# An MLP with more block products, every instruction in a planned order, 23 shared weight buffers, and sums and residual in DRAM

## The chip, the cores and the metric

The program runs on one core of a Trainium2 chip. The metric is the device time of the whole program in microseconds, as a median of several runs.

The engines are named as the profile names them: PE multiplies matrices, DVE (VectorE) and ACT (ScalarE) do elementwise work, POOL (GpSimd) does a little of it and can issue DMAs, and SP issues nearly all DMAs.

## What is computed

Two layers of a transformer with 256 tokens and width 2048. The attention parts (banded, stick-breaking and memory attention) are untouched by the change. The MLP of each layer is

```python
def sq_relu_mlp(h, g, w_in, w_out):
    return jnp.square(jax.nn.relu(rms_norm(h, g) @ w_in)) @ w_out

h = h + jnp.concatenate([y_main, y_mem], axis=-1) @ w_o[layer]
h = h + sq_relu_mlp(h, norm_mlp[layer], w_mlp_in[layer], w_mlp_out[layer])
```

with a hidden width of 8192. All data are float32.

## The kernel before

**Precision.** Each float32 factor is split into a part `hi` in PE's fp32r format and the rest, `lo`. A product is the sum of hi x hi, hi x lo and lo x hi. Each weight unit is a raw tile of 128 x 1024 that SP loads; ACT casts it to `hi` and DVE subtracts to get `lo` (`parts` L168, `prepare` L230). Pools give six raw, four hi and five lo buffers, and the units are prepared at most `AHEAD + 1` = 4 ahead of PE.

**The MLP in turns** (`mlp`, L985). The hidden width is cut into four chunks of 2048. PE's work is a list of steps (`mlp_steps`, L54, from the strings in `TURNS`):

- **U f** is one tile of 128 hidden features of the up product (`features_major`, L378 on): 16 wide matmuls (512 columns) with hi and 16 narrow ones (256 columns) with lo, into one PSUM bank. Then ACT copies the low half (L449), DVE adds (L1174), applies the relu and the norm (L1156), ACT squares (L1159), and the result is split into `hid`.
- **A j and B j** are direct steps of the down product, for one pair j of hidden tiles and one half (A or B) of a group's output columns: 12 wide matmuls each. They need one weight unit.
- **S j** does the work of A j and B j together by seven block products in place of eight (`Sevenfold`, `prepare_seven` L202, `Group.seven` L1084): 21 wide matmuls. For it, DVE forms block differences of the raw weights (L220 to L224, four of 512 columns) and of the hidden tile (`block_sums`, L1117), and ACT and DVE split four units, one of which is half as wide.

A group is one half of the output columns for a chunk: n = 0 or 1. The first three chunks have both groups in this form, the last one only n = 0; its other two column blocks are plain down products after it (L1240). `SEVEN = 5`: five of the eight pairs of every group are S steps, three are A and B.

A group holds seven of the eight PSUM banks until its sums are complete; one is left for U steps. When a bank is complete, `Group.add` (L1066) adds it to a sum in SBUF: an addition of 512 columns on DVE (L1082), or an ACT copy in the first chunk (L1080). At the end `merged` (L1016) adds the product sums to the four output sums of the group with six additions, and `turned` (L999) transposes the result on PE and adds it to the residual `h`, which stays in SBUF from the first out projection to the end. In the second layer the transposes of column block 3 come first, soon after the last S, A and B steps.

**What sets the order.** PE's order is the program's. On the other engines the framework's scheduler places the instructions by its own estimate, so a step's preparation runs beside earlier steps. Persistent tiles, heads and sums share a pool of 13 buffers (`grp`, L129).

The functions that the change touches, and those that call them:

Of the kernel before, what the change touches and what calls it, by code (L numbers as in the profile page):

```python
# [9 lines left out]
F32 = mybir.dt.float32  # L10
# [27 lines left out]
AHEAD = 3  # L38

# [14 lines left out]
def mlp_steps():  # L54

    steps = [(0, 0, "H", 0)] + [(0, 0, "T", f) for f in range(FIRST_UP, ALONE, 2)]
    for c in range(NCH):
        for n in range(2 if c < NCH - 1 else 1):
            for step in TURNS[n].split():
                kind, i = step[0], int(step[1:])  # L60
                steps.append((c + 1 if kind == "U" and n == 1 else c, n, kind, i))
    return steps


class InOrder:
# [5 lines left out]
    def __getattr__(self, name):  # L71
        fn = getattr(self._engine, name)

        def call(*args, **kwargs):
            return self._tc.keep_in_program_order(fn(*args, **kwargs))  # L75

        return call

# [17 lines left out]
class Engines:  # L96
    def __init__(self, tc):
        nc = tc.nc
        self.tensor = InOrder(tc, nc.tensor)
        self.vector, self.scalar, self.gpsimd, self.sync = nc.vector, nc.scalar, nc.gpsimd, nc.sync  # L100
# [3 lines left out]
def trunk(  # L104
# [97 lines left out]
    def prepare_seven(i, seven):  # L202
# [19 lines left out]
        elif seven.step == 3:  # L222
            nc.vector.tensor_tensor(b11, b22, b11, op=ALU.add)  # L223
            nc.vector.tensor_tensor(b21, b21, b11, op=ALU.subtract)  # L224
# [345 lines left out]
    def normed_heads(banks, eps_ms, gain, dst, wait=2):  # L570
# [24 lines left out]
        def side():  # L595
# [3 lines left out]
            for m in range(2):  # L599
# [11 lines left out]
                )  # L611

# [11 lines left out]
    def heads4(name):  # L624
        return grp.tile([P, 1024], F32, name=name, tag="g4")

# [156 lines left out]
    def load_tokens(src, name, queue):  # L783
        chunks = []
        for c in range(4):
            t = heads4(f"{name}{c}")
            pin(queue.dma_start(t[:], src[c]))
            chunks.append(t)
# [28 lines left out]
    def mlp_stream(l):  # L817
# [5 lines left out]
        for c, n, kind, i in mlp_steps():  # L823
# [115 lines left out]
    km, vm = [], []  # L939

    for l, mg in enumerate((mg0, mg1)):
# [10 lines left out]
        def keys(b, wait, k_=k_, g=g):  # L952

            late = 2 + wait
            later(lambda: normed_heads(b, mstat["em"], sm[:, g : g + 1], k_[:], late), wait)
# [10 lines left out]
        else:  # L966
            tokens_major(mg, lambda b: keys(b, 0))
            tokens_major(mg, lambda b: value_heads(b, mstat["r"], vm[1]))
# [16 lines left out]
    def mlp(l, xg_, sq, h, done):  # L985
        start_side(delayed(inverse_root(sq, f"mlp{l}"), 4))
        sums = [heads4(f"d{l}_{i}") for i in range(4)]
# [5 lines left out]
        extra = [heads4(f"e{l}_{i}") for i in range(3)]  # L993

        def product_sum(i, n):

            return extra[i][:, n * 512 : (n + 1) * 512]
# [18 lines left out]
        def merged(n):  # L1016

            u, p5, p7 = (product_sum(i, n) for i in range(3))
            for i, (dst, src) in enumerate((
                (summed(0, 2 * n + 1), u),  # L1020
                (summed(0, 2 * n + 1), p5),
                (u, p7),
                (summed(1, 2 * n), u),
                (u, p5),
                (summed(1, 2 * n + 1), u),
            )):
                pin(nc.vector.tensor_tensor(dst, dst, src, op=ALU.add))
# [10 lines left out]
        sevens = SEVEN  # L1038

        class Group:  # L1040

            def __init__(self, c, n, factors, staged=None):
                self.c, self.factors, self.staged = c, factors, staged
                self.banks = {}
# [5 lines left out]
                self.sums_of = {  # L1050
                    "11": [summed(0, 2 * n)], "21": [summed(1, 2 * n)],
                    "12": [summed(0, 2 * n + 1)], "22": [summed(1, 2 * n + 1)],
                    "p1": [product_sum(0, n), summed(0, 2 * n)], "p6": [product_sum(0, n)],
                    "p5": [product_sum(1, n)], "p7": [product_sum(2, n)],
                }
# [10 lines left out]
            def add(self, q, a, w):  # L1066
                count = self.counts[q]
                product(self.bank(q), a, w, count)
                if count[0] < count[1]:
                    return  # L1070
                src = self.banks[q][:]
                if self.staged is not None and q in ("12", "22", "p1", "p5", "p6", "p7"):

                    copy = wide.tile([P, 512], F32, name="copy", tag="wide")
                    nc.scalar.copy(copy[:], src)
                    self.staged.extend((dst, copy[:]) for dst in self.sums_of[q])
                    return
                for dst in self.sums_of[q]:
                    if self.c == 0 and q not in ("11", "p6"):
                        nc.scalar.copy(dst, src)  # L1080
                    else:
                        nc.vector.tensor_tensor(dst, src, dst, op=ALU.add)  # L1082

            def seven(self, j):  # L1084
                s = self.factors[j]
                width["last"] = "wide"
                for step, pairs in enumerate((
                    (("p1", s[0]), ("11", tokens(2 * j + 1, 0))),
                    (("12", s[4]),),
                    (("p5", s[1]), ("p7", s[3])),  # L1090
                    (("p6", s[2]), ("21", tokens(2 * j + 1, 1))),
                )):
                    w = weights()
                    for k2, (q, a) in enumerate(pairs):
                        self.add(q, a, part(w, k2))
                    if step in (1, 3):
                        slot()

            def direct(self, j, col):
                width["last"] = "wide"  # L1100
                w = weights()
                for m in range(2):
                    for k2 in range(2):
                        self.add(f"{m + 1}{col}", tokens(2 * j + k2, m), part(w, k2))
                slot()
# [11 lines left out]
        def block_sums(c, j, a, b):  # L1117

            whole = c == NCH - 1
            s23 = nar.tile([P, T], F32, name="s23", tag="nar")  # L1120
            s14 = nar.tile([P, T], F32, name="s14", tag="nar")
            a11, a21, a12, a22 = a[:, :P], a[:, P:], b[:, :P], b[:, P:]
            s1 = s14[:, :P] if whole else a21
            w = wide.tile([P, 512], F32R, name="s_w", tag="wide")
            if not whole:
                x = nar.tile([P, T], F32R, name="s_x", tag="bias", bufs=6)
                last = (x[:, :P], x[:, P:], s14[:, P:])
            elif j < 2:
                x = wide.tile([P, 512], F32R, name="s_x", tag="wide")
                last = (x[:, :T], x[:, T:], s14[:])  # L1130
            else:
                x = [nar.tile([P, T], F32R, name="s_x", tag="bias", bufs=6) for _ in range(2)]
# [298 lines left out]
```

## Time and profile before

| | us |
|---|---|
| median of 3 runs (2158.17 to 2159.33) | 2158.41 |
| the profiled execution | 2158.02 |
| its span, first to last instruction | 2156.3 |
| PE busy | 2148.9 |
| DVE busy | 1745.1 |
| ACT busy | 1248.3 |
| POOL busy | 205.5 |

The granted PE clock is 1.00 over the whole span. In the profile's rows a line such as L174 is the place in the kernel that issued the instruction, `out<-in` are the program's tiles, `x32` the count; after the bar stand the busy time of the group, the mean of one in ns, and the time that the engine was idle just before them with what ended the idle time. In a row of windows every engine has its busy time in that stretch with its number of instructions. All matmuls have one line, L75, since a helper issues them: the tiles tell them apart. Those of U read `mlpx`, those of the down product `hid`, `s_w` and `s_x`.

### The profile page before, as it was taken

The page shows a single profiled execution, that of the slowest core. Times are in us where ns is not written, and L with a number is a line of the kernel's source. Part 1 is how long each engine was busy: PE and PEld are TensorE (multiplying, and loading weights), DVE is VectorE, ACT ScalarE, POOL GpSimd, SP SyncE. Part 2 cuts the span into 40 slices and gives each one's busy share as a digit, 9 for nine tenths or more (in the row PEclk, how much of TensorE's full clock was granted, in tenths as well). Part 3 has the DMA queues.
Part 4 walks back from the last instruction along what each step waited for, and adds up shares of the span by engine and source line. Part 5 has one row for each costly group of instructions (what it writes and reads, how often), then busy time and mean ns, then how long its engine had stood idle before and what let it go on. Part 6 is the DMA issues. An engine that isn't in the chain of part 4 may idle for free.

```text
span 2156.3 us, 30341 instructions
## 1 busy us (share of the span) xinstructions
PE 2148.9 (100%) x11038; PEld 1841.2 (85%) x11038; DVE 1745.1 (81%) x2603; ACT 1248.3 (58%) x1828; POOL 205.5 (10%) x223
## 2 busy tenths in 40 slices
PE   9999999999999999999999999999999999999999
PEld 8888888888888888888888889888888888888887
DVE  7778885679898899989986556566988888988995
ACT  7744545556666566566555547655666656556663
POOL 0010112610000000000050112252000000000000
PEclk9999999999999999999999999999999999999999
DMA  9655556656666756666766654455666666666674
GB/s 331 193 165 187 167 180 195 196 188 187 192 200 200 214 180 197 205 199 196 215 177 194 187 187 137 131 184 184 185 214 186 197 205 200 202 194 205 186 224 128
DMA packets 213317, 414.65 MB, mean 192 GB/s; under 512 B 13232, under 2 KB 144304, under 8 KB 213168
## 3 DMA queue, kind: packets, MB, share of 16 engines
q1 hardware_dynamic: 212592, 410.63, 62.0%
q8 instruction: 86, 1.41, 0.3%
q10 hardware_dynamic: 576, 2.10, 0.3%
q14 instruction: 63, 0.52, 0.1%
HBM read 410.58 MB, written 2.10 MB: 191 GB/s over the span
## 4 chain that ended last, share of the span: by engine, by line
PE 98%; DVE 2%; issue 0%; ACT 0%; DVEq 0%
PE acc L75 93%; PE accs L75 1%; PE yp L75 1%; PE tp L75 1%; PE s L75 1%; PE z L75 1%; DVE lo L226 0%; PE cold L75 0%; DVE lo L174 0%; DVE pt L654 0%; DVE lo L248 0%; ACT hi L171 0%; DVE h L1011 0%; PE stat L75 0%; DVE raw L223 0%
## 5 line engine op out<-in xcount | busy, mean ns | idle before, releaser
L174 DVE TENSOR_TENSOR lo<-raw,hi 128x1024 fp32r<-128x1024 f32 (+1 forms) x524 | 642.5, 1237 | 220.9 <-ACT hi L171 194.8
L171 ACT CAST hi<-raw 128x1024 fp32r<-128x1024 f32 (+1 forms) x524 | 539.2, 1045 | 339.2 <-PE acc L75 286.0
L75 PE MATMUL acc<-mlpx,hi 128*128 128x512 f32 x2048 | 483.9, 389 | 0.0
L75 PE MATMUL acc<-hi,hid 128*128 128x512 f32 x1404 | 474.4, 391 | 0.0
L75 PEld LDWEIGHTS acc<-mlpx,hi 128*128 128x128 f32 x2048 | 383.6, 188 | 79.3
L225 ACT CAST hi<-raw 128x1024 fp32r<-128x1024 f32 (+1 forms) x280 | 264.8, 946 | 204.9 <-DVE raw L221 132.8
L226 DVE TENSOR_TENSOR lo<-raw,hi 128x1024 fp32r<-128x1024 f32 (+1 forms) x280 | 302.0, 1087 | 34.6 <-ACT hi L225 29.5
L75 PEld LDWEIGHTS acc<-hi,hid 128*128 128x128 f32 x1404 | 264.0, 188 | 52.6
L75 PE MATMUL acc<-lo,hid 128*128 128x512 f32 x702 | 274.5, 391 | 0.0
L75 PEld LDWEIGHTS acc<-mlpx,lo 128*128 128x128 f32 x2048 | 261.3, 191 | 9.0
L75 PE MATMUL acc<-mlpx,lo 128*128 128x256 f32 x2048 | 264.6, 283 | 0.0
L75 PE MATMUL acc<-hi,xg 128*128 128x512 f32 x640 | 208.4, 398 | 0.0
L75 PEld LDWEIGHTS acc<-lo,hid 128*128 128x128 f32 x702 | 132.3, 188 | 23.2
L247 ACT CAST hi<-raw 128x1024 fp32r<-128x1024 f32 x108 | 113.4, 1055 | 65.2 <-PE acc L75 54.6
L449 ACT COPY low<-acc 128x256 f32<-128x256 f32 x188 | 69.4, 369 | 136.1 <-PE acc L75 135.0
L75 PEld LDWEIGHTS acc<-hi,xg 128*128 128x128 f32 x640 | 120.2, 188 | 24.6
L248 DVE TENSOR_TENSOR lo<-raw,hi 128x1024 fp32r<-128x1024 f32 x108 | 131.0, 1230 | 6.1 <-ACT hi L247 6.1
L75 PE MATMUL acc<-lo,xg 128*128 128x512 f32 x320 | 124.7, 390 | 0.7 <-DVE lo L174 0.7
L75 PE MATMUL acc<-y,hi 128*128 128x512 f32 x512 | 119.9, 391 | 0.0
L75 PEld LDWEIGHTS acc<-y,hi 128*128 128x128 f32 x512 | 95.0, 188 | 19.1
L75 PE MATMUL acc<-hi,s_w 128*128 128x512 f32 x280 | 97.6, 389 | 0.0
L1159 ACT ACTIVATE up<-up 128x256 f32<-128x256 f32 x128 | 52.8, 415 | 40.2 <-DVE up L1156 40.2
(211 smaller groups left out, 2612.6 us busy)
## 6 DMA issues: line engine op xcount, KB each, us to landing
raw<-in_w_up SPq DMA_DIRECT2D x256, 512.0 KB, 4.8
raw<-in_w_down SPq DMA_DIRECT2D x256, 512.0 KB, 6.0
raw<-in_w_in SPq DMA_DIRECT2D x80, 512.0 KB, 3.9
raw<-in_w_o SPq DMA_DIRECT2D x64, 512.0 KB, 4.2
raw<-in_w_mem SPq DMA_DIRECT2D x28, 512.0 KB, 5.8
raw<-in_w_kv_v SPq DMA_DIRECT2D x24, 512.0 KB, 4.1
raw<-in_w_kv_k SPq DMA_DIRECT2D x24, 512.0 KB, 4.4
raw<-in_w_q SPq DMA_DIRECT2D x24, 512.0 KB, 4.2
```

What stands on the lines that cost most here:

```text
L75: return self._tc.keep_in_program_order(fn(*args, **kwargs))
L171: nc.scalar.copy(hi[:, :n], raw[:, :n])
L174: nc.vector.tensor_tensor(lo, raw, hi.bitcast(F32), op=ALU.subtract)
L225: nc.scalar.copy(hi4, src)
L226: nc.vector.tensor_tensor(lo4, src, hi4.bitcast(F32), op=ALU.subtract)
L247: nc.scalar.copy(hi4, turned)
L248: nc.vector.tensor_tensor(lo4, turned, hi4.bitcast(F32), op=ALU.subtract)
L449: nc.scalar.copy(low[:], bank[:, T:])
L1159: nc.scalar.activation(a[:], a[:], AF.Square)
```

## The change

**More block products.** `SEVEN` is now a table: seven pairs of eight in the first three chunks of both layers, five in the last. The turns for seven are `U S0 U S1 ... U S6 A7 B7` and the like. In each layer six groups have 7 S, 1 A and 1 B in place of 5 S, 3 A and 3 B. Nine U steps (before: ten) come ahead of the first S.

**An order planned by deadlines.** From the first of these steps to the last, nothing is issued as the code meets it. Each instruction becomes a `Job` with an engine, a cost, a due time and what it waits for. `in_turn` walks through the plan: PE, POOL and SP take their jobs in order; ACT and DVE take the job with the earliest due time among those that are ripe. The jobs are then issued in that order and every engine is held to it (`nc.use(nc.tied)`).

**23 shared buffers.** A raw, hi or lo tile no longer has its own pool: six raw, four hi, five lo and eight more buffers from `grp` serve any of the three. The half-wide unit of an S step keeps hi and lo in one buffer.

**Sums and residual in DRAM.** A complete bank is copied to SBUF by ACT. Two such copies fill a tile, which POOL sends by DMA to its sum in DRAM, adding there from the second chunk on. In the last chunk POOL brings the eight sums back into eight of the shared buffers, and DVE adds the last banks to them; `merged` has eight additions now. The residual goes to DRAM after each out projection and comes back in the last chunk; the second layer's memory keys and values do the same between their making and their use. `grp` has nine buffers instead of thirteen, and a second tag of four (`h4`) holds the residual or the copies.

The core of the diff:

```diff
-SEVEN = 5
-ALONE = 10
-TURNS = (
-    "U10 S0 U11 S1 U12 A5 S2 U13 S3 U14 A6 S4 U15 B5 B6 A7 B7",
-    "U0 S0 U1 A5 U2 S1 U3 A6 U4 S2 U5 A7 U6 S3 U7 S4 U8 B5 U9 B6 B7",
-)
+SEVEN = [[7, 7, 7, 5], [7, 7, 7, 5]]
+ALONE = 9
+TURNS = {
...
+    7: (
+        "U S0 U S1 U S2 U S3 U S4 U S5 U S6 A7 B7",
+        "U S0 U S1 U S2 U S3 U S4 U S5 U S6 U A7 U B7",
+    ),
+}
...
+def in_turn(jobs, slots, counts, reserve=RESERVE):
...
+    queues = {e: [job for job in jobs if job.engine == e] for e in ("PE", "POOL", "ACT", "DVE", "SP")}
+    for e in ("ACT", "DVE"):
+        queues[e].sort(key=lambda job: job.key)
...
+                look = queue[:1] if e in ("PE", "POOL", "SP") else queue[:160]
+                job = next((x for x in look if can(x, now)), None)
...
-    grp = ctx.enter_context(tc.tile_pool(name="grp", bufs=13))
+    grp = ctx.enter_context(tc.tile_pool(name="grp", bufs=9))
...
+    away = ctx.enter_context(tc.tile_pool(name="away", bufs=10, space=bass.MemoryType.DRAM))
...
+    def put_away(tile_, name):
+
+        home = away.tile([P, 1024], F32, name=f"away_{name}", tag="away")
+        nc.gpsimd.dma_start(home[:], tile_[:])
+        return home
...
-                for dst in self.sums_of[q]:
-                    if self.c == 0 and q not in ("11", "p6"):
-                        nc.scalar.copy(dst, src)
-                    else:
-                        nc.vector.tensor_tensor(dst, src, dst, op=ALU.add)
...
+            def copy_out():
+                if (id(homes), k) not in g.copies:
+                    g.copies[id(homes), k] = kept4("copy")
+                i = place(q, n)[1]
+                nc.scalar.copy(
+                    g.copies[id(homes), k][:, i * 512 : (i + 1) * 512], g.banks[q][:]
+                )
...
+            def send():
+                if c == 0:
+                    nc.gpsimd.dma_start(out=homes[k][:], in_=g.copies[id(homes), k][:])
+                else:
+                    nc.gpsimd.dma_start(
+                        out=homes[k][:], in_=g.copies[id(homes), k][:], accum_op=ALU.add
+                    )
...
+        slots = [("g4", m) for m in range(SPARE)] + [("raw", m) for m in range(6)]
+        slots += [("hi", m) for m in range(n_given, 4)] + [("lo", m) for m in range(n_given, 5)]
+        counts = {"acc": 4, "t": 1, "y": 1, "nar": 6, "wide": 7, "bias": 6, "copy": COPIES, "s": 2}
...
+        order = in_turn(jobs, slots, counts)
+        nc.use(nc.tied)
+        for job in order:
+            job.emit()
+        nc.use(nc.free)
```

Three places show how instructions move. The first is DVE shortly after the planned part begins in the first MLP. Before (`raw` and `lo` are weight tiles, `up<-acc` takes the bank of a U step, `4x128` is a block difference of weights):

```order
L1174 TENSOR_TENSOR up<-acc,low 128x256
L226 TENSOR_TENSOR lo_4814<-raw_0_4710,hi_4813 128x1024
L174 TENSOR_TENSOR lo_4829<-raw_4827,hi_4828 128x1024
L1156 SCALAR_TENSOR_TENSOR up<-up,ri_mlp_4388 128x256
L174 TENSOR_TENSOR lo_4839<-raw_4837,hi_4838 128x1024
L1115 TENSOR_TENSOR s_x<-s_4753,s_x 128x128
L226 TENSOR_TENSOR lo_4856<-raw_0_4851,hi_4855 128x1024
L226 TENSOR_TENSOR lo_4869<-raw_1_4853,hi_4868 128x512
L1115 TENSOR_TENSOR hid_4160<-up,hid_4160 128x256
L220 TENSOR_TENSOR raw_1_4853<-raw_1_4853 128x4x128
L221 TENSOR_TENSOR raw_1_4853<-raw_1_4853,raw_0_4851 128x4x128
L223 TENSOR_TENSOR raw_0_4851<-raw_1_4853,raw_0_4851 128x4x128
```

Now, up to the lo that the last product of S1 needs (`raws`, `his`, `los` and `g4s` are the shared buffers, each of which may hold a raw, a hi or a lo tile):

```order
L194 TENSOR_TENSOR s_4843<-up 128x128
L194 TENSOR_TENSOR hid_4175<-up,hid_4175 128x256
L194 TENSOR_TENSOR s_4864<-up,s_4843 128x128
L194 TENSOR_TENSOR g4s_1_4866<-g4s_4_4680,los_0_4812 128x1024
L194 TENSOR_TENSOR s_w<-s_4843,s_w 128x256
L194 TENSOR_TENSOR s_x<-s_4864,s_x 128x128
L194 TENSOR_TENSOR g4s_4_4680<-g4s_5_4682,g4s_4_4680 128x4x128
L194 TENSOR_TENSOR g4s_4_4680<-g4s_4_4680 128x4x128
L194 TENSOR_TENSOR up<-acc,low 128x256
L194 TENSOR_TENSOR los_1_4906<-g4s_5_4682,his_1_4890 128x1024
L194 TENSOR_TENSOR his_2_4913<-g4s_6_4684,g4s_0_4826 128x1024
L194 TENSOR_TENSOR g4s_1_4923<-g4s_4_4680,los_0_4911 128x1024
```

The lo units of U and S no longer come in the order of the steps but mixed, and the block differences of the hidden tile (`s`, `up` with 128 columns) stand between block differences of weights.

The second place is DVE at the end of the planned part of the second MLP, from the last banks of the direct steps on. Before (`d` and `e` are the sums in SBUF, `copy` a bank that ACT has copied; `h<-tp` comes soon after):

```order
L248 TENSOR_TENSOR lo_19943<-raw_19941,hi_19942 128x1024
L1082 TENSOR_TENSOR d_0_13872<-acc,d_0_13872 128x512
L1082 TENSOR_TENSOR d_2_13874<-acc,d_2_13874 128x512
L1027 TENSOR_TENSOR e_0_13876<-e_0_13876,e_1_13877 128x512
L1186 TENSOR_TENSOR d_0_13872<-d_0_13872,copy 128x512
L248 TENSOR_TENSOR lo_19965<-raw_19963,hi_19964 128x1024
L1027 TENSOR_TENSOR d_3_13875<-d_3_13875,e_0_13876 128x512
L1186 TENSOR_TENSOR d_0_13872<-d_0_13872,copy 128x512
L1186 TENSOR_TENSOR d_2_13874<-d_2_13874,copy 128x512
```

Now, from the second bank of A7 on (`sum` are the sums brought back from DRAM; one lo and the last addition to `sum_3` follow before the transposes):

```order
L194 TENSOR_TENSOR sum_2_20049<-acc,sum_2_20049 128x512
L194 TENSOR_TENSOR los_1_20398<-los_2_20338,los_0_20394 128x1024
L194 TENSOR_TENSOR sum_1_20240<-sum_1_20240,sum_2_20257 128x512
L194 TENSOR_TENSOR sum_3_20400<-sum_3_20400,sum_2_20257 128x512
L1406 TENSOR_TENSOR sum_0_19953<-sum_0_19953,copy 128x512
L194 TENSOR_TENSOR sum_1_20240<-sum_1_20240,sum_3_20400 128x512
L377 TENSOR_TENSOR lo_20432<-raw_20430,hi_20431 128x1024
L1406 TENSOR_TENSOR sum_2_20049<-sum_2_20049,copy 128x512
L194 TENSOR_TENSOR sum_1_20240<-sum_1_20240,sum_2_20257 128x512
L194 TENSOR_TENSOR sum_3_20400<-sum_3_20400 128x512
L194 TENSOR_TENSOR sum_3_20285<-sum_3_20285,sum_3_20400 128x512
L194 TENSOR_TENSOR sum_3_20400<-sum_3_20400,sum_2_20257 128x512
```

Most of the merge of the four product sums stands behind these banks now, and the transposes that read the result come after it.

The third place is POOL between the last out projection's work and the end of the first MLP. Before, no instruction of POOL lies in the MLP: squares of the residual (`sq`, `mlpsq`) are followed by those after the MLP (`kvsq`):

```order
L977 TENSOR_TENSOR low_4145<-low,h_3211 128x256
L481 TENSOR_TENSOR sq<-h_3211 128x256
L482 TENSOR_TENSOR mlpsq_3214<-mlpsq_3214,sq 128x256
L553 TENSOR_TENSOR root<-ms,neg_half 128x4
L478 TENSOR_TENSOR kvsq<-h_3205 128x256
L481 TENSOR_TENSOR sq<-h_3205 128x256
L482 TENSOR_TENSOR kvsq<-kvsq,sq 128x256
L481 TENSOR_TENSOR sq<-h_3205 128x256 x2
L482 TENSOR_TENSOR kvsq<-kvsq,sq 128x256 x2
L481 TENSOR_TENSOR sq<-h_3207 128x256 x2
```

Now (`away` is the residual in DRAM, `d` and `e` are the sums in DRAM, `copy` a pair of banks):

```order
L764 DMA away_h_3_4165<-h_3217 128x1024
L611 TENSOR_TENSOR mlpsq_3220<-mlpsq_3220,sq 128x256
L682 TENSOR_TENSOR root<-ms,neg_half 128x4
L194 DMA e_0_4171<-copy 128x1024
L194 DMA e_1_4172<-copy 128x1024
L194 DMA d_0_4167<-copy 128x1024
L194 DMA d_2_4169<-copy 128x1024
L194 DMA e_2_4173<-copy 128x1024
L194 DMA e_3_4174<-copy 128x1024
L194 DMA d_1_4168<-copy 128x1024
L194 DMA d_3_4170<-copy 128x1024
L194 DMA e_0_4171<-copy 128x1024
```

Eight DMAs per chunk stand in POOL's queue, and after them those that bring the residual and the sums back.

More of the change, by code (lines that the diff above doesn't have):

```diff
@@ L1 @@
+import heapq
 from collections import deque
@@ new lines, with __init__ @@
+CAST = {128: 300, 256: 405, 512: 623, 1024: 1053}
+SUM = {128: 280, 256: 415, 512: 685, 1024: 1222}
+LOW, SQUARE, COPY = 370, 415, 596
+OVERLAP = {"DVE": 85, "ACT": 75}
+TOLD = 60
+WIDE, NARROW, DRAIN = 227, 120, 200
+ISSUE = {"SP": 60, "POOL": 860}
+LANDS, MOVES, ADDS = 3400, 1690, 2600
+SOON = 200
+class Job:
+    def __init__(self, engine, cost, emit, key, after=(), take=0, give=(), get=(), free=(), adds=False, kinds="g4 raw hi lo"):
+        self.engine, self.cost, self.emit, self.key = engine, cost, emit, key
+        self.after = [job for job in after if job is not None]
+        self.take, self.give, self.get, self.free = take, give, get, free
+        self.adds, self.begun, self.told = adds, None, None
+        self.slots, self.tiles, self.kinds = [], [], kinds.split()
@@ L1066, in add @@
             def add(self, q, a, w):
[L1067 to L1077, printed above, removed]
-                for dst in self.sums_of[q]:
-                    if self.c == 0 and q not in ("11", "p6"):
-                        nc.scalar.copy(dst, src)
-                    else:
[L1082 to L1105, printed above, removed]
+                product(self.bank(q), a, w, self.counts[q])
         def tokens(kt, m):
@@ new lines, in add_job @@
+        def add_job(*args, **kwargs):
+            job = Job(*args, **kwargs)
+            jobs.append(job)
+            return job
+        costs = {"U": 16 * (WIDE + NARROW), "S": 21 * WIDE, "A": 12 * WIDE, "B": 12 * WIDE}
+        begins, now = [], 0
+        for _, _, kind, _ in steps:
+            begins.append(now)
+            now += costs[kind]
+        begins.append(now)
+        next_up = [
+            next((begins[m] for m in range(k + 1, len(steps)) if steps[m][2] == "U"), begins[-1])
+            for k in range(len(steps))
+        ]
@@ new lines, in add_slots, with pe @@
+        def add_slots(*slots):
+            return Held(list(slots))
+        groups = {}
+        ready_at = {}
+        last_pe, bring = None, []
+        alone = min(SEVEN[l][0], ALONE // 2)
+        held = {(0, m): ["wide", "bias"] for m in range(alone)}
+        merge = merged(1)
+        def pe(cost, emit, key, after, give=(), get=(), free=()):
+            nonlocal last_pe
+            last_pe = add_job("PE", cost, emit, key, after, give=give, get=get, free=free)
+            return last_pe
@@ new lines, in mlp @@
+            count([q for q, _ in pairs], end + 2500)
+            if (c, kind, i) == (NCH - 1, "B", KT // 2 - 1):
+                before = None
+                for m in range(4):
+                    after = [returned[id(hs), kk] for hs, kk in sum_homes[4:]]
+                    before = add_job(
+                        "DVE", 2 * SUM[512], lambda: next(merge, None), begins[k] - 9000 + 3000 * m,
+                        [*after, before],
+                    )
+                add_job("POOL", 0, lambda: bring_h(3), begin, [before], get=("copy",))
```

650 lines of the change are left out of this document (555 added, 95 removed).

## The prediction

> **What bounds the kernel now.** First the page's busy shares and its chain of waits, then TensorE's own waits.
>
> ```profile
> PE 2148.9 (100%) x11038; PEld 1841.2 (85%) x11038; DVE 1745.1 (81%) x2603; ACT 1248.3 (58%) x1828; POOL 205.5 (10%) x223
> PE 98%; DVE 2%; issue 0%; ACT 0%; DVEq 0%
> PE tp L75 <- DVE h L1011: 2.2, 2, 1.1
> PE cold L75 <- DVE zeros L142: 1.1, 1, 1.1
> PE acc L75 <- DVE lo L174: 0.7, 1, 0.7
> ```
>
> PE is never without work: 4.0 us of waits in the whole run, and the chain that ends last is PE for 98%. A matmul taken away shortens the run by its interval, as long as PE still finds its operands ready. The intervals are read from PE's timeline inside the first MLP: a U step is one feature tile of the up product, A5 a direct step, and what begins at 666.32 an S step.
>
> ```profile
> 641.49 3.79 PE L75 MATMUL acc<-mlpx,hi 128*128 128x512 f32 x16
> 645.11 2.08 PE L75 MATMUL acc<-mlpx,lo 128*128 128x256 f32 x16
> 647.02 0.40 PE L75 MATMUL acc<-hi,hid 128*128 128x512 f32 x1
> ...
> 649.77 3.79 PE L75 MATMUL acc<-mlpx,hi 128*128 128x512 f32 x16
> ...
> 666.32 0.40 PE L75 MATMUL acc<-hi,hid 128*128 128x512 f32 x1
> ...
> 671.11 3.79 PE L75 MATMUL acc<-mlpx,hi 128*128 128x512 f32 x16
> ```
>
> U takes 647.02 - 641.49 = 5.53 us, a direct step 2.75 us for 12 matmuls, an S step 4.79 us for 21. One wide matmul is 0.228 us.
>
> The next engine is DVE. One chunk period in the middle of the MLP, by windows and by groups within it:
>
> ```profile
> core 0: us, PE busy (x) PEld busy (x) DVE busy (x) ACT busy (x) POOL busy (x), PEclk, DMA share, GB/s
> 788.00:957.52 169.52, 169.52 (x868) 145.07 (x867) 155.04 (x221) 101.93 (x143) 0.00 (x0) 1.00 0.64 199
> L226 DVE TENSOR_TENSOR lo<-raw,hi 128x1024 fp32r<-128x1024 f32 x30 | 36.6, 1220 | 2.7 <-ACT hi L225 2.0 <-PE acc L75 0.5
> L248 DVE TENSOR_TENSOR lo<-raw,hi 128x1024 fp32r<-128x1024 f32 x12 | 14.4, 1218 | 0.0
> L221 DVE TENSOR_TENSOR raw<-raw,raw 128x512 f32<-128x512 f32 x10 | 6.9, 692 | 0.3
> L226 DVE TENSOR_TENSOR lo<-raw,hi 128x512 fp32r<-128x512 f32 x10 | 6.9, 686 | 0.9 <-ACT hi L225 0.8
> L1082 DVE TENSOR_TENSOR d<-acc,d 128x512 f32<-128x512 f32 x10 | 6.7, 684 | 1.0 <-PE acc L75 1.0
> L1082 DVE TENSOR_TENSOR e<-acc,e 128x512 f32<-128x512 f32 x8 | 5.4, 684 | 0.5 <-PE acc L75 0.5
> L1115 DVE TENSOR_TENSOR s_w<-s,s_w 128x256 fp32r<-128x256 f32 x5 | 2.1, 418 | 0.0
> L1140 DVE TENSOR_TENSOR s<-up,s 128x128 f32<-128x128 f32 x5 | 1.4, 287 | 0.0
> ```
>
> DVE works 155.0 of 169.5 us, 91%; a period has 16 U, 10 S and 12 direct steps. How DVE's records lie behind one another decides what is left, so its timeline:
>
> ```profile
> 861.89 2.36 DVE L174 TENSOR_TENSOR lo<-raw,hi 128x1024 fp32r<-128x1024 f32 x2
> 864.17 1.82 DVE L226 TENSOR_TENSOR lo<-raw,hi 128x1024 fp32r<-128x1024 f32 x2
> 866.02 0.69 DVE L220 TENSOR_TENSOR raw<-raw 128x512 f32<-128x512 f32 x1
> 866.75 0.69 DVE L221 TENSOR_TENSOR raw<-raw,raw 128x512 f32<-128x512 f32 x1
> ```
>
> Two independent 1024-wide subtractions start 1.14 us apart (861.89 to 864.17 for two) though each record is 1.22 us: independent neighbours overlap by 0.08 us. Those that touch each other's data don't (866.02 to 866.75, 0.73 us for a record of 0.69).
>
> **PE: what goes.** Per layer, six groups go from five S steps and six direct ones to seven and two: +12 S, -24 direct. An S costs 21 matmuls, the two direct steps that it replaces 24. So 24 x 3 = 72 matmuls of 0.228 us go: 16.4 us, all on the path. The order of PE's instructions has 72 matmuls less. The profiled execution took 2158.02 us (0.4 below the median 2158.41): 2158.0 - 16.4 = 2141.6 if nothing new waits.
>
> **DVE: what it has to do in the shorter period.** Four S more: each three 1024-wide subtractions (1.220), one 512-wide (0.686) and four block differences (0.69), 7.11 us, together +28.4. Eight direct units less: 8 x 1.218 = -9.7. All 18 additions of L1082 go, since ACT now copies the banks out and DMAs add in DRAM: -12.3. Two pairs more of block sums of the hidden tile, each four 128-wide at 0.287 and two splits of 0.418 and about 0.287: +3.7. Sum +10.1; of the 18 instructions more some overlap, -0.9: DVE needs about 164.2 us in a period of 169.5 - 12 x 0.228 = 166.8 us, 98%. That is the weak point: 2.6 us of slack instead of 14.5. Six such periods run (three chunks, two layers).
>
> In the middle of the MLP I price this at nothing. The cover is the lead: by the order, where DVE takes the bank of a U step, the next lo that it has not yet made is used two PE steps, about 10 us, after that U; before, it was sometimes 3.6 us, in the same count.
>
> At the entry the lead is not yet built. From U8's bank to the lo of the last product of S1, DVE's order (the change, first place) has eight 1024-wide (1.14), ten 512-wide (0.61), eight 256-wide (0.34) and six 128-wide (0.2) instructions, 19.1 us with neighbours overlapped, some 0.5 us for those that don't overlap, and 0.7 us until the bank can be added: 20.3. PE passes U9, S0, U10 and 15 matmuls of S1 in 5.53 + 4.79 + 5.53 + 3.42 = 19.3 us, so it waits about 1.0 us, and by the same count about 0.9 more until the middle of the chunk. Taken: 1.9 us per layer, 3.8 in all; bounds 0 (DVE a little quicker than its rows) and 8 (twice that).
>
> At the end of the second MLP the transposes of group 3 follow two units after the last direct step. DVE must do fourteen instructions between A7's second bank and them (the change, second place): three at 1.14 and eleven at 0.61, 10.1 us, and some 0.4 for dependent ones; PE has 3 x 2.75 = 8.2 us. Before, five of them stood between. PE waits 2.4 us. In the first MLP the first transposes come after six units, 7 x 2.75 = 19.2 us behind that bank, and 22 instructions (six at 1.14, sixteen at 0.61, 1 us for dependent ones, 17.6) fit: 0. Taken: 2.4; bounds 0 and 8.
>
> **ACT.** It gains four S (three casts and a short one each), loses eight casts, and copies 16 banks.
>
> ```profile
> L225 ACT CAST hi<-raw 128x1024 fp32r<-128x1024 f32 x30 | 31.6, 1053 | 26.9 <-DVE raw L221 19.8 <-PE acc L75 4.4 <-DVE raw L224 2.4
> L225 ACT CAST hi<-raw 128x512 fp32r<-128x512 f32 x10 | 6.2, 624 | 3.4 <-PE acc L75 3.3
> L1080 ACT COPY d<-acc 128x512 f32<-128x512 f32 x4 | 2.4, 596 | 0.7 <-PE acc L75 0.7
> ```
>
> +4 x 3.78 - 8 x 1.06 + 16 x 0.596 = +16.2: about 118 of 166.8 us, 71%. Nothing on the path by itself; it matters only as DVE's supplier.
>
> **DMA and POOL.** Each period POOL issues 8 DMAs of 512 KB, mostly adding in DRAM, 4.2 MB beside the weights' 33.7 MB (199 GB/s x 169.5 us). The DMA share of 0.64 becomes 0.72 if an addition costs what its bytes cost, 0.88 if it costs three times that; below 1 at both ends. No row shows an adding DMA; the nearest are these loads:
>
> ```profile
> raw<-in_w_down SPq DMA_DIRECT2D x256, 512.0 KB, 6.0
> h<-in_x_t ACTq DMA_DIRECT2D x4, 512.0 KB, 5.8
> ```
>
> A weight load gets its buffer at least three PE steps (15 us) ahead of its first matmul, by the order, so a landing a few us later than 6.0 is hidden. An adding DMA that takes twice as long holds one of four copy buffers for 12 us of some 83 per group. I take 0, bounds 0 and 6. POOL works beside DVE in the out projections only, where DVE's records are longer:
>
> ```profile
> L463 DVE SCALAR_TENSOR_TENSOR mlpx<-h,sm,mlpx 128x256 fp32r<-128x256 f32 x32 | 21.8, 682 | 8.1 <-ACT mlpx L461 8.1
> L463 DVE SCALAR_TENSOR_TENSOR mg<-memc,sm,mg 128x256 fp32r<-128x256 f32 x32 | 14.4, 480 | 3.0 <-ACT mg L461 2.7
> ```
>
> If each of the 8 issues lengthened one DVE instruction by those 0.2 us, that is 1.6 us per period, still inside the slack. The residual and the second layer's memory keys and values go out and come back far from their use: 0.
>
> **The sum:** 2158.0 - 16.4 + 3.8 + 2.4 = 2147.8; I say 2148.
>
> **Rivals.**
>
> *All of it hidden.* DVE's entry and tail sums are a few per cent off and PE never waits: 2142. For it: PE waited 4.0 us in all at 91% DVE.
>
> *DVE becomes the bound.* In the period above DVE also idles, mostly for ACT:
>
> ```profile
> DVE lo L174 <- ACT hi L171: 4.9, 8, 1.3
> DVE lo L226 <- ACT hi L225: 2.8, 6, 0.6
> ```
>
> If these 7.7 us stay in the planned order, a period takes 164.2 + 7.7 = 171.9 us, 5.1 above PE's: 6 x 5.1 = 31, 2172, slower. It costs from 2.6 us of idle per period on, and the whole gain from 2.6 + 16.4 / 6 = 5.3. For it: a fixed order that mixes chains of ACT and DVE lets one late cast hold all behind it. Against: ACT is 29% idle and has 23 buffers to work ahead in.
>
> *The sums come back late.* Eight 512 KB loads of stored sums are issued by POOL in the last chunk; DVE's merge waits for them, and the lo of the next units stands behind the merge. If the last lands 4 us late in both layers: 2148 + 8 = 2156, no change. For it: the last is issued, by the order, three steps before the merge, against a landing of 6.0.
>
> *Records add up.* The Trainium skill, "VectorE: DVE Perf Modes", section "The DRAIN you can't avoid", says that the next DVE instruction does not start until the pipe is empty, so durations would add. As a mechanism here: the records of the period above sum to 166.2 us, those after to 166.2 + 10.1 = 176.3 against 166.8, 9.5 us per period, 57 in all: 2199. The timeline's 1.14 us for records of 1.22 speaks against it, so it gets 2%. (By that rule the kernel before would be near DVE's limit; the trace disagrees.)
>
> *It does not do what it says.* PE's order shows 72 matmuls less, so this has no chance worth a number.
>
> **How the numbers follow.** Forecast (2143 to 2154) 0.57, all hidden 0.16, late sums 0.12, DVE the bound 0.13, records add up 0.02. Of the late sums and of the mild end of the DVE bound some fall under 2154: +0.03 faster. Over 0.2% (4.3 us, about what a measurement of this kernel can tell from no change): faster 0.76, same 0.11, slower 0.13. The range takes the all-hidden case, the sums' upper bounds (2141.6 + 8 + 8 + 6 = 2164), and leaves out the worse half of the DVE bound: 2141 to 2164.
>
> **What would show it.** Right: a period between the same steps of two chunks takes 166.8 us; DVE is busy 97 to 98% of it; PE's waits name DVE's lo in the first half of the first chunk (2 us per layer) and DVE's sums before the transposes. Wrong: periods of 168 us or more with PE waiting for DVE's lo in each, DVE idle for ACT (DVE the bound); DVE waiting for the stored sums at the end of an MLP (late sums); no DVE overlap left (records add up).

## The result, and the profile after

The changed kernel takes 2181.92 us (median of 4 runs, 2179.71 to 2183.25) against 2158.66 beside it: ratio 1.0106, 95% interval 1.0094 to 1.0118. It is 1.1% slower, where 2148 was forecast (2141 to 2164). The profiled execution took 2179.71 us, its span 2177.9.

The page of the kernel after: busy shares, and the chain that ended last.

```profile
PE 2144.5 (98%) x10966; PEld 1827.2 (84%) x10966; DVE 1803.9 (83%) x2745; ACT 1308.2 (60%) x1968; POOL 259.7 (12%) x307
PE 77%; DVE 14%; DMA 5%; issue 3%; ACT 1%; SPq 0%; DVEq 0%; ACTq 0%
```

The 72 matmuls are gone (11038 to 10966), but the chain, 98% PE before, now runs through DVE for 14% and through DMAs for 5%. PE's own waits, before 4.0 us in all, are 26.0 now. The five largest groups:

```profile
PE acc L194 <- DVE up L194: 4.6, 4, 1.3
PE acc L194 <- DVE los L194: 4.4, 5, 1.5
PE tp L194 <- DVE hb L1178: 3.9, 2, 2.2
PE acc L194 <- DVE his L194: 3.8, 2, 1.9
PE tp L194 <- DVE sum L194: 2.7, 1, 2.7
```

All five are put down to DVE, and of the rest only 0.9 us to ACT. They don't say why DVE was late, and that turned out to be three different things. To find the places, each step of PE is compared with its undisturbed length (U 5.53, S 4.79, A and B 2.75 us), and what is over is summed by stretch over both layers. "Entry" runs from U8 to the last B of the first chunk's first group, "middle" is the groups from there to the end of the third chunk, "last" the fourth chunk's; then the time between the MLPs (last planned step to U8), PE's time from the last planned step of the second MLP to its last matmul, and from there to the end of the span:

| us | entry | middle | last | between | PE's tail | end |
|---|---|---|---|---|---|---|
| before | 0.5 | 1.1 | -0.2 | 436.7 | 48.9 | 3.2 |
| after | 11.2 | 15.5 | 2.5 | 440.4 | 52.2 | 6.6 |
| light | 2.9 | 13.3 | -0.1 | 441.1 | 52.2 | 6.6 |
| store | 11.1 | 2.2 | -0.1 | 442.8 | 50.6 | 6.6 |
| nosend | 11.0 | 1.8 | -0.1 | 442.3 | 52.4 | 4.0 |
| light_store | 2.9 | 0.3 | -0.1 | 441.6 | 52.8 | 6.6 |
| merge_light | 11.1 | 19.3 | 2.3 | 438.9 | 47.6 | 6.6 |
| quiet | 11.1 | 17.1 | 2.9 | 442.8 | 52.8 | 3.4 |
| closed | 2.4 | 1.1 | -0.1 | 438.4 | 47.6 | 3.4 |
| sooner | 8.6 | 15.7 | 2.5 | 441.7 | 52.9 | 6.6 |
| adds52 | 11.1 | 14.1 | 3.2 | 446.1 | 48.6 | 6.6 |
| five | 6.1 | -0.3 | 5.8 | 444.2 | 54.4 | 6.6 |
| six | 7.0 | 0.5 | 4.5 | 439.3 | 47.9 | 6.6 |
| six_all | 4.4 | 0.6 | 4.8 | 439.2 | 47.9 | 3.4 |
| mix_all | 8.5 | 2.7 | 6.1 | 441.4 | 52.2 | 3.4 |
| before6 | 6.4 | 34.3 | 3.4 | 436.7 | 55.6 | 3.2 |

After against before: 10.7 + 14.4 + 2.7 + 3.7 + 3.3 + 3.4, and 0.5 ahead of the first MLP, are 38.7 us. The spans say 2177.9 - (2156.3 - 16.4) = 38.0; the rest is rounding of the step lengths. Each row is one execution; the columns "between" and "PE's tail" differ by up to some 2 us even between versions that change nothing there (between: 440.4 to 442.8 in after, light, store, sooner and quiet), so small differences in them mean little.

### The profile page after: what moved, and what is told of

It reads as the page before. It is cut to its first block, busy times and chain, and to the rows that moved or that the text cites. A ratio compares the mean times of both kernels' runs of the same rounds, so it can differ in the third digit from the quotient of the medians.

```text
span 2177.9 us, 30420 instructions
## 1 busy us (share of the span) xinstructions
PE 2144.5 (98%) x10966; PEld 1827.2 (84%) x10966; DVE 1803.9 (83%) x2745; ACT 1308.2 (60%) x1968; POOL 259.7 (12%) x307
## 4 chain that ended last, share of the span: by engine, by line
PE 77%; DVE 14%; DMA 5%; issue 3%; ACT 1%; SPq 0%; DVEq 0%; ACTq 0%
PE acc L194 73%; DVE g4s L194 4%; DVE raws L194 2%; DVE los L194 2%; DVE his L194 2%; DMA his<-in_w_down 2%; DMA raws<-in_w_down 1%; PE accs L194 1%; PE yp L194 1%; DVE up L194 1%; DMA los<-in_w_down 1%; DMA g4s<-in_w_down 1%; PE tp L194 1%; PE s L194 1%; PE z L194 1%
## 5 line engine op out<-in xcount | busy, mean ns | idle before, releaser
L304 DVE TENSOR_TENSOR lo<-raw,hi 128x1024 fp32r<-128x1024 f32 (+1 forms) x308 | 382.7, 1251 | 180.1 <-ACT hi L301 153.0
L301 ACT CAST hi<-raw 128x1024 fp32r<-128x1024 f32 (+2 forms) x308 | 318.8, 1039 | 274.2 <-PE acc L194 228.0
L194 PE MATMUL acc<-mlpx,g4s 128*128 128x256 f32 (+1 forms) x1024 | 190.1, 333 | 0.0
L194 PE MATMUL acc<-mlpx,raws 128*128 128x512 f32 (+1 forms) x960 | 183.2, 336 | 2.0 <-DVE up L194 2.0
L194 PEld LDWEIGHTS acc<-mlpx,g4s 128*128 128x128 f32 x1024 | 161.4, 190 | 21.4
L194 PE MATMUL acc<-g4s,hid 128*128 128x512 f32 x504 | 173.9, 392 | 1.4 <-DVE hid L194 1.1
L194 PEld LDWEIGHTS acc<-mlpx,raws 128*128 128x128 f32 x960 | 153.3, 189 | 24.3 <-DVE up L194 3.2
L194 PE MATMUL acc<-raws,hid 128*128 128x512 f32 x430 | 150.8, 394 | 2.2 <-DVE hid L194 1.3
L194 PE MATMUL acc<-mlpx,los 128*128 128x512 f32 (+1 forms) x720 | 146.7, 350 | 0.0
L194 PE MATMUL acc<-mlpx,his 128*128 128x256 f32 (+1 forms) x752 | 137.6, 328 | 2.6 <-DVE up L194 2.6
```

Source lines behind the costliest of these rows:

```text
L301: nc.scalar.copy(hi[:, :n], raw[:, :n])
L304: nc.vector.tensor_tensor(lo, raw, hi.bitcast(F32), op=ALU.subtract)
```

## The experiments

Theory D: DVE has too little room. Theory L: weight loads land late behind the adding DMAs. Theory O: the pinned order itself loses time. All times below are medians, with the kernel before at 2158.5 to 2158.7 beside them.

### DVE's load and the adding DMAs

light forms the block differences on a quarter of the columns, so its products are not those of the MLP; the planned order stays as it stood:

```diff
             def minus(out, x, y, op=ALU.subtract):
-                nc.vector.tensor_tensor(out(), x(), y(), op=op)
+                nc.vector.tensor_tensor(out()[:, :1], x()[:, :1], y()[:, :1], op=op)
```

> The planned order is kept as it is, but each of the four block differences of an S step works on 128 of its 512 columns (so the products of S are not those of the reference). It takes about 0.4 us from each of 376 DVE instructions, 22 us of a period of 14 S steps, and nothing from PE, ACT or any DMA. DVE saturated (its work fills the period, so every lag stays): the 30 us that PE loses in the planned parts nearly go, 2145 to 2155 us. Late weight loads beside the adding DMAs: DVE was not the cause, 2172 or more. The pinned order itself (instructions standing behind one that waits for a buffer): some of it goes, 2162 to 2178.

2167.94 us. D promised more: 14 us came back, not 30. The time alone would also fit O (2162 to 2178). The table shows which stretch gained: the entry falls from 11.2 to 2.9, the middle stays at 13.3. The entry by windows, of the kernel after and of light:

```profile
480.00:575.00 95.00, 91.54 (x464) 76.32 (x463) 93.61 (x146) 66.36 (x101) 2.21 (x4) 1.00 0.66 211
```

```profile
480.00:575.00 95.00, 94.37 (x482) 79.87 (x481) 85.40 (x153) 69.09 (x107) 2.21 (x4) 1.00 0.66 217
```

The columns are the stretch, then PE, weight loads, DVE, ACT and POOL busy, PE's clock, the DMA share and GB/s. After, DVE is busy 93.61 of 95 us: it was simply behind. With 85.40 PE runs through. So D holds at the entry, and not in the middle. (The last chunk's 2.5 us go with this edit and also with the next two.)

nosend, the adding DMAs of the second and third chunk left out (the `else` of `send`), and store, with plain stores in their place; in both the sums are incomplete:

```diff
-                    nc.gpsimd.dma_start(
-                        out=homes[k][:], in_=g.copies[id(homes), k][:], accum_op=ALU.add
-                    )
+                    nc.gpsimd.dma_start(out=homes[k][:], in_=g.copies[id(homes), k][:])
```

> The adding DMAs of the second and third chunk are left out (32 of 512 KB, 16 per layer, so the sums lack two chunks); copies, order and buffers stay as planned. DVE saturated: nothing changes, 2178 to 2183 us. Late weight loads beside the adding DMAs: loads land in 6 us again instead of 9, and 10 to 25 us come back, 2157 to 2172. Pinned order: 2176 to 2183.

> The 32 DMAs of the second and third chunk store their copies instead of adding them to the sums (so the sums hold the last chunk stored, not the total); the same bytes are sent, nothing is read in DRAM. Theory: it is the adding that stretches the weight loads queued behind it to 20 us, so most of what nosend gained comes back: 2164 to 2170 us. Rival: it is the bytes, and nothing changes: 2178 to 2183.

2163.25 and 2164.13 us: L in both. The middle falls from 15.5 to 1.8 and 2.2, the entry stays. Not the bytes but the adding costs nearly all of that time. How, is seen in the third chunk's head. ACT's timeline, of the kernel after and of store:

```profile
744.71 1.05 ACT L194 CAST his<-g4s 128x1024 fp32r<-128x1024 f32 x1
752.02 0.62 ACT L194 CAST los<-los 128x512 fp32r<-128x512 f32 x1 [6.26 <-PE acc L194]
752.55 1.05 ACT L194 CAST raws<-los 128x1024 fp32r<-128x1024 f32 x1
```

```profile
744.22 1.05 ACT L194 CAST his<-g4s 128x1024 fp32r<-128x1024 f32 x1
746.69 0.62 ACT L194 CAST los<-los 128x512 fp32r<-128x512 f32 x1 [1.42 <-DMA los<-in_w_down]
747.22 1.05 ACT L194 CAST raws<-los 128x1024 fp32r<-128x1024 f32 x1
```

The same cast waits 6.26 us in one and 1.42 in the other. After, the row names PE; store names the load. The issues and landings show that it is the load in both. After (us; in brackets the time to landing, then that of the same load in store and in nosend):

```
SP   729.87 -> 750.61 (20.73; 14.98; 10.36) his<-in_w_down
SP   731.72 -> 751.94 (20.22; 15.51; 10.12) los<-in_w_down
POOL 729.70 -> 741.52 (11.82) e<-copy     POOL 731.29 -> 744.53 (13.24) e<-copy
POOL 736.43 -> 747.44 (11.01) d<-copy     POOL 737.07 -> 750.43 (13.36) d<-copy
```

The cast begins at 752.02, 0.08 us after its load has landed. Four sends under way make the loads beside them 5 us later here when they store, 10 us later when they add. In the second MLP the same two loads take 20.3 and 19.6 us after, 17.0 and 16.6 in store, 9.3 and 9.4 in nosend.

Both loads are those of S2. Its first matmul comes at 763.83, 34 us after the first issue, so they land 12 to 13 us ahead of it and still cost time. The reason is the fixed order: the half-wide cast of S2 (752.02) stands ahead of S1's last cast (752.55), and S1 is what PE works on then. One late load holds the casts behind it, which were due sooner. From there it goes on: DVE idles 5.4 us for ACT, PE waits 1.3 us for a bank and 1.9 for a lo, and then the clock halves (0.50 granted from 771 to 773). PE's timeline there, S2's first matmul and the wait:

```profile
763.83 0.40 PE L194 MATMUL acc<-raws,hid 128*128 128x512 f32 x1
...
767.26 0.39 PE L194 MATMUL acc<-los,s_w 128*128 128x512 f32 x1
769.53 0.75 PE L194 MATMUL acc<-his,s_w 128*128 128x512 f32 x1 [1.89 <-DVE his L194]
770.08 0.63 PE L194 MATMUL acc<-los,s_w 128*128 128x512 f32 x1
770.51 0.63 PE L194 MATMUL acc<-los,hid 128*128 128x512 f32 x1
```

After the wait a matmul takes 0.43 us, start to start, in place of 0.228. The heads of the third chunk in both layers lose 9 of the middle's 15.5 us; its other places were not followed row by row.

light_store is both edits in one:

> light and store in one: block differences on 128 of 512 columns, and stores in place of adding DMAs (products and sums are not the reference's). If DVE's load and the adding DMAs are all that the planned part loses, 28 of the 30 us there go and what is left are the waits at the ends of the MLPs and POOL's drain: 2141.6 + 10 to 12: 2151 to 2154 us. If the two share one loss (late loads only hurt since DVE has no room), little is gained over store: 2158 to 2163. If the pinned order loses time by itself, as much.

2155.69 us, ratio 0.9986 (0.9977 to 0.9995). Entry 2.9, middle 0.3, last -0.1: the two together remove nearly all that the planned parts lose, in the same pinned order. It is 2 to 5 us above the forecast, since the ends cost more than I had put down.

### The plan and its order

free leaves out `nc.use(nc.tied)`; adds52 sets `ADDS` from 2600 to 5200.

> The jobs are issued in the planned order, but ACT, DVE, POOL and SP are not held to it: the framework's scheduler places them by its own estimate. Theory (DVE saturated at the entry, loads late behind adding DMAs): an order of another kind neither takes DVE's work away nor brings the loads earlier: 2172 to 2195 us. Rival (the pinned order is the cause, one late cast holding all behind it): 2150 to 2168.

> The planner is told that an adding DMA holds the queue for 5.2 us instead of 2.6 (in the trace two of them made the loads behind them 10 us later, 5 us each); it plans another order from that. Theory: the loss at the head of the third chunk comes from loads that the plan expects 10 us earlier than they land, so part of the 15 us between the second and the fourth chunk comes back: 2170 to 2178 us. Rival (there is no room for a later load anywhere, whatever is planned): 2179 to 2186.

free took 2286.67 us, far worse than any theory had it: the planned order is worth some 100 us here. With light_store, which keeps that order and loses hardly anything in the planned parts, O falls as a cause of its own. The order only passes a late load on, as seen above. adds52 took 2181.24: another plan moves the loss within the middle and leaves it at 14.1. Its premise was off, too: counted over all four sends under way, an addition costs the loads some 2.6 us, which the planner had.

early has U6 and U7 planned as well (`range(FIRST_UP, ALONE - 3, 2)` for the steps ahead of the plan); sooner finishes the first four hidden tiles at `began + 8 + f` in place of `began + 11 + f`.

> The planned part of each MLP begins three U steps ahead of the first S step's neighbours instead of one (U6 and U7 join the plan), so DVE has two U steps, 11 us, more in which to get ahead of S0 and S1. Theory: the 5.6 us that each layer loses from S0 to A7 of the first group are DVE's backlog at the entry, as in light, where they fell to 1.5; 2181.9 - 8 to - 11: 2170 to 2174 us. Rival: over a whole period DVE has no room, so the backlog only comes out later: 2179 to 2184.

> The relu, squares and block sums of the first four hidden tiles of an MLP are issued three slots earlier, ahead of the planned part (where DVE is 88% busy) and no longer in its first 15 us; plan, order and the work of the planned part stay. That takes some 12 DVE instructions, 3 us, from between the planned part's start and S0. Theory (DVE is behind at the entry by its amount of work): S0 and S1 wait 1.8 and 1.3 us less each or nearly so; 2 x 2 to 2 x 3 us: 2176 to 2178 us, and S0 to A7 lose 2.5 to 3.5 us per layer instead of 5.6. Rival (the entry waits for casts or loads, as in early): 2180 to 2184.

early took 2187.34 us, outside both forecasts: S0 alone is 8.7 us late in each layer. Around it, in early:

```profile
490.00:500.00 10.00, 5.22 (x29) 3.90 (x27) 9.62 (x21) 8.05 (x15) 0.00 (x0) 0.98 0.05 5
```

Until 493 DVE works on the block sums of the first hidden tiles, and hardly a weight is loaded (DMA share 0.05). The edit made a new jam, so it says nothing about backlog. sooner moves the same block sums out of the way: 2180.19 us, in its rival's range by the time. In the trace S0's excess falls from 1.83 to 0.51 us, S1's stays at 1.26, so a quarter of the entry is gone, less than forecast.

### More or fewer pairs

five and six change only `SEVEN` (5 everywhere; 6, 6, 6, 5). six_all is six with sooner and quiet, mix_all the same with 7, 6, 6, 5. before6 is the kernel before with six pairs:

```diff
-SEVEN = 5
+SEVEN = 6
-    "U10 S0 U11 S1 U12 A5 S2 U13 S3 U14 A6 S4 U15 B5 B6 A7 B7",
-    "U0 S0 U1 A5 U2 S1 U3 A6 U4 S2 U5 A7 U6 S3 U7 S4 U8 B5 U9 B6 B7",
+    "U10 S0 U11 S1 U12 S2 U13 S3 U14 A6 S4 U15 S5 B6 A7 B7",
+    "U0 S0 U1 S1 U2 A6 U3 S2 U4 A7 U5 S3 U6 S4 U7 S5 U8 B6 U9 B7",
```

> Six pairs in place of seven in the first three chunks, all else as in the changed kernel. PE has 36 matmuls more, 8.2 us. DVE saturated: a period asks 7 us less of DVE, 157 of 169 us, and the lost time mostly goes: floor 2149.8, 2151 to 2160 us. Late loads or the pinned order: what is lost stays, 2181.9 + 8.2 less a few us: 2180 to 2190.

> Five pairs everywhere, as before the change, in the new machinery (planned order, shared buffers, sums and residual in DRAM). PE has the matmuls of the kernel before. DVE saturated: DVE has less to do than in the kernel before (no additions of banks), so 2157 to 2163 us. Late loads: the DMAs are the same, 2170 to 2185. Pinned order: 2170 to 2195.

> Six pairs in place of seven, POOL's last additions on DVE (as in quiet), and the first four hidden tiles finished earlier (as in sooner). If the gains add: 2166.5 - 3.4 - 2 x 2.5 = 2158 us, 2156 to 2161; floor 2149.8. It says whether the new machinery can reach the kernel before at all.

> Seven pairs in the first chunk, whose sums are stored and not added, six in the second and third, with quiet and sooner. Floor 2149.8 - 2.7 = 2147. Theory (adding DMAs hurt only where DVE has no room, in the second and third chunk): 2.7 us less than six_all or a little worse for the longer entry: 2156 to 2160 us. Rival (seven pairs cost the loss wherever they stand): 2163 to 2170.

> The kernel before with six pairs in place of five, its own turns and nothing of the new machinery: bank sums added by DVE in SBUF, no DMA from POOL. PE has 48 matmuls less in three chunks and the last one of two layers (14 half groups, 3 each: 9.6 us less): floor 2149. DVE's period: 155.0 + 2 x 7.1 - 4 x 1.2 + 1.9 = 166.3 of 168.2 us, 99%. Theory (a DVE at 98% or more can't be kept ahead): it loses 10 to 25 us, 2159 to 2175. Rival (the loss is all in adding DMAs and the plan): 2149 to 2156, faster than the kernel before.

six took 2166.54 us, between the forecasts; five 2183.55, where only the rivals of D had it. Both have the same 48 sends, and their middle loses 0.5 and nothing: with six pairs or fewer late loads cost PE nothing there. They land as late as with seven: in six one took 22.6 us, and the cast behind it waited 3.6 us, PE not at all. Whether it is a longer lead or DVE's greater room that hides this was not separated; light, with room on DVE and seven pairs, kept its 13.3 us. five, with the matmuls of the kernel before, is 25 us slower than that kernel: entry, last chunk, both ends and the drain. That is what the new machinery costs without a gain.

six_all took 2160.61, ratio 1.0009 (1.0000 to 1.0018), as forecast, and no better than the kernel before. mix_all took 2168.46, in the rival's range; its middle is indeed quiet (2.7), but entry, last chunk and both ends lose 12 us more than in six_all. Why a plan with seven pairs in the first chunk is worse at the far end of the MLP is open. before6 took 2199.44, worse than forecast (its PE has 42 matmuls less, 11038 to 10996, not 48). Its PE waits:

```profile
PE acc L75 <- DVE lo L226: 13.7, 20, 0.8
PE acc L75 <- DVE hid L1115: 7.1, 6, 1.6
PE acc L75 <- ACT hid L1114: 4.8, 4, 1.2
```

Without plan, shared buffers and DMAs from POOL, one pair more, in these turns, already loses 51 us over its floor (2158.0 - 42 x 0.228 = 2148.4). With six pairs the changed kernel's machinery is 33 us faster than that (six).

### The ends, and the sum

merge_light narrows the additions of `merged` and of the staged banks to 128 columns, so the sums are incomplete; quiet gives POOL's additions in the second MLP's last products to DVE; closed joins light, store, sooner, quiet and merge_light.

```diff
-                dst, src = home_of(dst, n), home_of(src, n)
+                dst, src = home_of(dst, n)[:, :P], home_of(src, n)[:, :P]
...
-            nc.gpsimd.tensor_tensor(h(o), h(o), t[:], op=ALU.add)
+            (nc.vector if l == 1 else nc.gpsimd).tensor_tensor(h(o), h(o), t[:], op=ALU.add)
```

> The changed kernel with only the merge's additions narrowed to 128 of 512 columns (16 at the end of each MLP, 0.4 us less each, with those of the copied banks 20). Theory (DVE stands behind the merge at both ends of MLP): PE's waits at the transposes shrink, 4 to 8 us less: 2174 to 2178 us. Rival (late loads for the units there): 2179 to 2184.

> In the second MLP's last plain down products the additions of POOL go to DVE, so POOL's last instruction is the DMA that brings back the residual, some 50 us before the end. Theory: the drain at the end of POOL's program (7.73 us, against 0.83 in the kernel before; 5.12 where 32 DMAs are left out, so 0.082 us for each DMA that POOL has issued) begins after POOL's last instruction and no longer ends last: 3.4 us less, 2178 to 2179 us, and the span ends about 1 us after the last store has landed. Rival: the drain begins only when the whole program ends, or DVE's two or more additions are in the way: 2181 to 2184.

> light_store with three things more: POOL's last additions on DVE (quiet), the first four hidden tiles finished earlier (sooner), and the merge's additions of the sums on 128 of 512 columns (its result is not the reference's). If the account is complete, 2155.7 - 3.4 (drain) - 2 x 1 (entry) - 4 to 8 (the waits at the ends of the MLPs) = 2142 to 2146 us, the floor of 2141.6 nearly reached. If something else in the new machinery costs time (loads for the plain down products, the residual's way out and back), 2148 or more.

merge_light took 2176.82 us, as the theory had it: PE's tail falls from 52.2 to 47.6 us, below the kernel before, the time between the MLPs from 440.4 to 438.9. It is the merge in this plan: six has the whole merge, a tail of 47.9 us and no such wait. Of the waits for the residual's additions (`hb`) in the first MLP, 3.9 us after and 1.1 before, 2.6 stay in merge_light and in closed; what they come from is open. The windows of the kernel after show what the wait for the merge (2.7 us) costs beside itself:

```profile
2124.00:2126.00 2.00, 0.59 (x4) 0.19 (x2) 1.72 (x3) 1.71 (x2) 0.00 (x0) 1.00 0.96 379
2126.00:2128.00 2.00, 0.75 (x5) 0.71 (x6) 2.00 (x3) 0.28 (x1) 0.00 (x0) 1.00 0.39 61
2128.00:2130.00 2.00, 2.00 (x7) 1.56 (x6) 0.93 (x2) 0.00 (x0) 0.00 (x0) 0.53 0.69 244
2130.00:2132.00 2.00, 2.00 (x7) 1.48 (x7) 0.00 (x0) 0.00 (x0) 0.00 (x0) 0.62 0.73 242
2132.00:2134.00 2.00, 2.00 (x12) 1.73 (x11) 0.69 (x1) 1.05 (x1) 0.00 (x0) 1.00 0.43 109
```

The clock falls to 0.53 and 0.62 (the column behind POOL's), and 7 matmuls pass in 2 us where 9 would.

quiet took 2177.07 us, 1 us better than forecast; its end is 3.4 us after the last matmul, near the 3.2 before. closed took 2144.56, ratio 0.9934 (0.9920 to 0.9947), within its forecast, 3 us above the floor of 2141.6. Its page:

```profile
PE 2132.2 (100%) x10966; PEld 1827.0 (85%) x10966; DVE 1658.0 (77%) x2749; ACT 1303.0 (61%) x1968; POOL 245.3 (11%) x303
PE 98%; DVE 1%; DMA 0%; issue 0%; ACT 0%; SPq 0%; DVEq 0%; ACTq 0%
```

The account nearly closes: DVE's load, which light lowers everywhere but which cost time at the entry, the additions in DRAM, the merge and POOL's drain are all but 3 us of the loss. No version that computes all of it beat the kernel before.

## Why the prediction was wrong, step by step

- **PE, 16.4 us less: right.** Where the loads come in time, a period takes nearly what was forecast, 166.6 us in store against 166.8. The kernel after and store, by windows, from U9 of the second chunk to U9 of the third:

```profile
658.26:830.27 172.01, 168.80 (x855) 143.84 (x854) 158.33 (x235) 111.80 (x167) 6.20 (x8) 0.99 0.72 214
```

```profile
657.77:824.38 166.61, 166.61 (x856) 142.85 (x854) 160.96 (x240) 114.19 (x170) 4.25 (x8) 1.00 0.71 226
```

- **DVE in the period, 98%: nearly right, and harmless in itself.** In store DVE works 161.0 of 166.6 us, 97% (forecast 164.2, 3 us too much), and PE waits for nothing in that stretch. The rival "DVE becomes the bound" would have been the reading of the kernel after, period 172.0 (171.9 in that rival) and waits for DVE in it. That match is luck: the other periods behind the first chunk take 168.9, 170.4 and 170.3. light and store say otherwise, too: less DVE work leaves the middle at 13.3 us, stores in place of additions bring it to 2.2.
- **DMA, 0 with bounds 0 to 6: the step that failed.** "A weight load gets its buffer at least three PE steps (15 us) ahead of its first matmul, by the order, so a landing a few us later than 6.0 is hidden." Two things in it were wrong. The landing was not a few us later than 6.0 but 20 us beside additions. And the lead to the first matmul is not the cover: in the place shown above it was 34 us, and the load landed 12 us ahead of its first matmul, but its cast stood in ACT's order ahead of one that was due sooner. Landings of 15 to 17 us (store) cost nearly nothing. I had said that no row showed an adding DMA and took its bounds from plain loads; 14.4 us in the middle came of it, more than twice the upper bound. That takes the gain of 16.4 us almost whole. The median landings after, in the page's list of DMA issues:

```profile
g4s<-in_w_up SPq DMA_DIRECT2D x76, 512.0 KB, 9.1
g4s<-in_w_down SPq DMA_DIRECT2D x75, 512.0 KB, 8.7
e<-copy POOLq DMA_DIRECT2D x24, 512.0 KB, 11.2
d<-copy POOLq DMA_DIRECT2D x24, 512.0 KB, 8.3
```

- **The entry, 1.9 us per layer: right in kind, a third of its size.** It lost 5.4 per layer more than before. I counted from U8's bank on to one lo of S1 and gave S0 nothing; S0 waits first:

```profile
493.73 0.39 PE L194 MATMUL acc<-his,hid 128*128 128x512 f32 x1
495.64 0.50 PE L194 MATMUL acc<-los,hid 128*128 128x512 f32 x1 [1.52 <-DVE los L194]
```

- **The transposes of the second MLP, 2.4 us: the wait was 2.7.** Left out were the 1.6 us at half clock behind it (with 1.1 of waits that were there before, the tail is 3.3 longer), and the first MLP, which I priced at 0 and which lost 3.7 with the stretch to the next one.
- **Late sums: no cost.** No wait of DVE names the stored sums. They come back in 6.1 to 6.4 us by the medians. The last in the first MLP takes 10.3, more than the rival's 4 us too late, and still lands at 1072.5, 8 us ahead of the merge's first addition (1080.4).
- **Records add up: refuted again.** DVE's records in store's period sum to 177.6 us, and the period takes 166.6. The rival took only half of what it cites. The Trainium skill, "VectorE: DVE Perf Modes", section "The DRAIN you can't avoid", says that the next instruction waits for the pipe to empty, and goes on that one that is not held starts earlier. The rows agree with the second half: starts 1.14 us apart for records of 1.22.
- **The end: not seen.** 3.4 us of POOL's drain stand in no step of mine.

With what was measured, the sum reads 2141.6 + 14.4 + 10.7 + 2.7 + 3.7 + 3.3 + 3.4 + 0.5 = 2180.3, against 2179.7 for the profiled execution.

## What to carry to other kernels

When work is moved to an engine or a queue that the profile shows idle, price what it does to the transfers beside it, and compare the landing of the loads under that traffic, not the landing shown before, with the turn of their casts in the order, not with their first matmul. Nearly all of PE's waits named DVE here, and DVE's own work was the cause at the entry and at the merge, not in the middle: an experiment that lightens the named engine alone tells whether it is late or is made late. A wait of PE can cost more than its length, and a tight plan has such waits at its two ends first, where no lead has been built or where everything comes due at once.

## What was unexpected of the hardware

- **POOL's drain at the end is longer the more DMAs POOL has issued.** Its long DRAIN record took 0.83 us in the kernel before (no DMA), 5.12 in nosend (52) and 7.73 in the kernel after (84): 0.082 us for each, if the count is what it goes by; these three counts are all there are. In quiet, where it begins beside the last DMA issue and not some 67 us behind it, the record takes 11.37 us, off the path. In the kernel after it begins at POOL's last instruction (2169.39), and the program ends behind it: 4.4 us after the last store has landed, against 1.0 before and 1.2 in quiet.
- **The clock halves after waits of about 2 us, but not after each.** In the kernel after, seven matmuls ran at half rate after a wait of 1.9 us at 769.5 and eight after 2.7 us at 2127.2, 1.4 and 1.6 us lost; a wait of 1.9 us at 1809.1 and one of 2.2 at 1108.5 cost nothing more. The Trainium skill, "TensorE: Matmul & The Clock Gate", section "What's actually happening", tells of a free-running window of about 3.4 us that must pass idle. That it runs free fits the differing outcomes; that a wait of 2 us is enough does not fit.
- **Adding in DRAM costs the loads beside it more than storing the same bytes does**: behind four sends of 512 KB, 10 us in place of 5 in the first MLP, 10 to 11 in place of 7 to 8 in the second.
